# One core, two-layer encoder: the seventh product of a fast feed-forward chunk placed behind the second of the next

## The chip, the cores and the metric

The kernel runs on one core of a Trainium2 chip. The metric is device microseconds of one execution, from the reference's inputs in HBM to the output in HBM.

## What is computed

Two encoder layers on 1024 tokens of width 1024, all in float32. Each layer is a modulated RMS norm, an attention block with a gated residual, a second modulated RMS norm and a SwiGLU feed-forward block with a gated residual. What the change touches is the second half of a layer:

```python
def swiglu(h, w_in, w_out):
    gate, up = jnp.split(h @ w_in, 2, axis=-1)
    return (jax.nn.silu(gate) * up) @ w_out

x = x + gate2 * swiglu(h, f_w_in[i], f_w_out[i])     # h: 1024 x 1024, w_in: 1024 x 5632, w_out: 2816 x 1024
```

After layer 0 the next layer's first norm follows, after layer 1 the final norm.

## The kernel before, in words

**Arithmetic.** A float32 operand is held as a rounded half and the rest (`split`, L95): ScalarE casts the tile to its rounded half (L96), VectorE subtracts that from the tile (L97). A product of two operands is three TensorE matmuls (`mm3`, L99: hi x hi at L106, hi x lo at L107, lo x hi at L108), each over 512 columns. Activations are stored with the features on the partitions, so that a weight block is the stationary operand and 512 tokens are the moving one.

**First feed-forward matmul** (`ffn`, L847). Of the 22 chunks of 128 gate and 128 up features, the first two (LEAD) are computed directly by `plain` (L922), once for each half of the tokens, with four products of 12 matmuls each. The other 20 are computed by `fast` (L934), which takes both halves of the tokens at once with seven products of 12 matmuls instead of eight (a Strassen scheme: the four quarters are token half by half of the contraction against gate or up). A chunk so has 84 matmuls. The seven moving operands `ops[1..7]` are formed once by `norm_parts` (L754); the seven weight operands are formed for each chunk by `w_operands` (L806): four raw blocks of 128 x 512 come by DMA, named (1,1), (1,2) for gate and (2,1), (2,2) for up; GpSimd forms sums and differences of them (`comb`, L816, L817), and each operand is then split into a pair `whi`, `wlo`. Pool `rw` has 5 raw tiles (RAW), pool `rp` 4 pairs (RP). The difference for product 7 is written into a raw tile of its own (L825), so that a chunk takes five raw tiles; the other sums are written over a block.

**The order inside `fast`** is 1, 7, 6, 2, 5, 4, 3. Products 1, 6, 5, 3 are summed one after the other in one half of a PSUM tile "S" (two of them exist), 7 and 4 in its other half, 2 in a bank "T". Between them the running sum is read out: after 1 by ScalarE (L941), after 7 by ScalarE (L943), after 6 by ScalarE (L945), after 2 by VectorE (L947), after 5 by VectorE (L952), after 4 by VectorE (L954), after 3 by ScalarE with Silu (L958). `glu` (L917, L919) multiplies gate and up, and `keep` (L891) stores the results and, for every second chunk, four differences of them to `gd` in HBM (seven stores, L895, for two chunks). In layer 0 a step of the next layer's modulation (`ada_half`, L138: a raw tile by DMA, L148 on ScalarE, L150 on GpSimd, and row sums on TensorE at each end of eight) is put in after product 2 and after product 4.

**What sets the order on each engine.** Each engine works through its own queue in order. The queues' order is fixed when the program is built, by a scheduler that walks a simulated time: among the instructions that are ready it takes the one earliest in the program's text. `high_priority(offset=n)` lets an instruction count as n places earlier. Forming and splitting a weight operand has it (WAHEAD, 60); the read-outs L941 to L958 and the Silu and product of `plain` (L931, L919) have none. A tile of a pool is given out again when its last reader is done.

**Second feed-forward matmul.** Seven such products again (`product`, L1021), in the order 1, 2, 6, 7, 4, 5, 3, each over 11 slices of 12 matmuls; a slice loads and splits a weight block (`left`, L986) and an activation tile from `gd` (`right`, L1010). After product 4 the first token half is complete. `norm(0, ...)` (L1046) is called there, ahead of product 5: `norm_rb` (L195) sums the squares over the partitions with row sums on TensorE (L187), raises them to the power -1/2 on GpSimd (L203) and spreads them with TensorE again (L193). What remains of the norm (8 steps in layer 0, each L214, L216, L217; 4 in layer 1, `final`, L1096) is kept in `side`, and one is taken after every second slice.

Of the kernel before, what the change touches and what calls it, by code (L numbers as in the profile page):

```python
# [11 lines left out]
AF = mybir.ActivationFunctionType  # L12
ALU = mybir.AluOpType
AX = mybir.AxisListType

P = 128
S = 1024
# [3 lines left out]
CH = 512  # L21
# [10 lines left out]
EAHEAD = 60  # L32
# [7 lines left out]
NP = NF // 2  # L40
# [19 lines left out]
class Trunk:  # L60
# [38 lines left out]
    def mm3(self, ps, w, xs, n, w0=0, first=True, last=True, more=False):  # L99

        whi, wlo = w
        mm = self.nc.tensor.matmul
        for k in range(n):
            ws = slice((w0 + k) * P, (w0 + k + 1) * P)
            xh, xl = xs[k]
            mm(ps, lhsT=whi[:, ws], rhs=xh, start=first and k == 0 and not more, stop=False, skip_group_check=more)  # L106
            mm(ps, lhsT=whi[:, ws], rhs=xl, start=False, stop=False, skip_group_check=more)  # L107
            mm(ps, lhsT=wlo[:, ws], rhs=xh, start=False, stop=last and k == n - 1, skip_group_check=more)  # L108

    def mm_part(self, ps, w, xs, part):  # L110
        n = KT // PARTS
# [80 lines left out]
        for i in range(n):  # L192
            nc.tensor.matmul(ps[:, i * P:(i + 1) * P], lhsT=r[:, i:i + 1].to_broadcast([P, P]), rhs=self.ident, start=True, stop=True)  # L193

    def norm_rb(self, sq, n=4, ps=None):  # L195
        nc = self.nc
        if ps is None:
            ps = self.bank("A")
        self.rowsum(ps, sq, n)
        v = self.t(self.sp, "v8", [P, 4])  # L200
        nc.vector.tensor_scalar(out=v[:, :n], in0=ps[:, :n], scalar1=1.0 / D, scalar2=EPS, op0=ALU.mult, op1=ALU.add)
        r = self.t(self.sp, "r8", [P, 4])
        nc.gpsimd.tensor_tensor(out=r[:, :n], in0=v[:, :n], in1=self.nhalf[:, :n], op=ALU.pow)  # L203
        self.bcast(ps, r[:, :n], n)
        return ps

    def norm_apply(self, pool, xs, rb, av, bv, hs):
# [598 lines left out]
    def w_operands(self, layer, f):  # L806
# [12 lines left out]

        def get(i):  # L820
            hi, lo = self.w_pair()
            if i in (1, 2, 4, 8):
                t = blk(*{1: (1, 1), 2: (1, 2), 4: (2, 2), 8: (2, 1)}[i])
            elif i in (7, 9):
                t = self.t(self.rw, "raw", [P, CH])  # L825
                x, y = (blk(2, 1), blk(1, 1)) if i == 7 else (blk(1, 1), blk(1, 2))
            else:
                t = blk(2, 1) if i == 5 else blk(1, 1) if i == 6 else blk(1, 2)
                if i != 3:
                    x, y = blk(2, 1), blk(2, 2)  # L830
            with self.tc.high_priority(offset=WAHEAD):
                if i == 7:
                    comb(t, x, y, ALU.subtract)
                elif i == 9:
                    comb(t, x, y, ALU.add)
                elif i == 5 and 6 not in raw:
                    comb(t, x, y, ALU.add)
                elif i == 6:
                    raw[6] = comb(t, comb(x, x, y, ALU.add), t, ALU.subtract)
                self.split(hi, lo, t)  # L840
                if i == 2 and 6 in raw:
                    comb(t, t, raw[6], ALU.subtract)
            return hi, lo

        return get

    def ffn(self, layer, wo, xdst):  # L847
        nc, tc, a = self.nc, self.tc, self.a
        m = self.mods[layer]
        gate2 = m[5]  # L850
        with tc.tile_pool(name="hb", bufs=22, reuse_waits="tile") as hb, \
# [22 lines left out]
            for c in range(2):  # L874
                sq = wo.part_b(ft, wslot, c, todo)
# [9 lines left out]
            tt = nc.vector.tensor_tensor  # L885
# [28 lines left out]
            def prod(ps, i, w):  # L914
                self.mm3(ps, w, ops[i], 4, first=i in (1, 2, 7), more=i in (3, 4, 5, 6))

            def glu(f, c, x, y):  # L917
                t = g_tile()
                tt(out=t, in0=x, in1=y, op=ALU.mult)  # L919
                return lambda: keep(f, c, t)  # L920

            def plain(f, c):  # L922

                get = self.w_operands(layer, f)
                ps = self.t(self.pss, "S")
                for h, (i, j) in enumerate((((1, 1), (2, 2)), ((8, 1), (4, 2))) if c == 0 else (((9, 3), (1, 7)), ((8, 7), (5, 3)))):
                    o = ps[:, h * CH:(h + 1) * CH]
                    self.mm3(o, get(i[0]), ops[i[1]], 4, last=False)
                    self.mm3(o, get(j[0]), ops[j[1]], 4, first=False)
                t = f_tile()  # L930
                nc.scalar.activation(out=t, in_=ps[:, :CH], func=AF.Silu)  # L931
                return glu(f, c, t, ps[:, CH:])

            def fast(f):  # L934

                get = self.w_operands(layer, f)
                xz, y = self.t(self.pss, "S"), self.bank("T")
                x, z = xz[:, :CH], xz[:, CH:]
                gate1, up1, gate0, up0 = (f_tile() for _ in range(4))
                prod(x, 1, get(1))  # L940
                nc.scalar.copy(out=gate0, in_=x)  # L941
                prod(z, 7, get(7))
                nc.scalar.copy(out=up1, in_=z)  # L943
                prod(x, 6, get(6))
                nc.scalar.copy(out=up0, in_=x)  # L945
                prod(y, 2, get(2))
                tt(out=gate0, in0=gate0, in1=y, op=ALU.add)  # L947
                nc.scalar.activation(out=gate0, in_=gate0, func=AF.Silu)
                if ada:
                    ada.pop(0)()  # L950
                prod(x, 5, get(5))
                tt(out=up1, in0=up1, in1=x, op=ALU.add)  # L952
                prod(z, 4, get(4))
                tt(out=up0, in0=up0, in1=z, op=ALU.add)  # L954
                if ada:
                    ada.pop(0)()
                prod(x, 3, get(3))
                nc.scalar.activation(out=gate1, in_=x, func=AF.Silu)  # L958
                a, b = glu(f, 0, gate0, up0), glu(f, 1, gate1, up1)
                a()  # L960
                b()

            for c in range(2):
                for f in range(LEAD):
                    plain(f, c)()
                if c == 0:
                    for s in late:
                        s()
            for f in range(LEAD, NF):
                fast(f)  # L970
            if layer == 0:
                self.make_a(self.avec[1][0], self.sm[:, C_N1 + 8:C_N1 + 16], self.mods[1][1])

# [3 lines left out]
            box = [{}, {}]  # L977
            hn = [[None] * KT, [None] * KT]
            side = []
# [30 lines left out]
            def right(i, k):  # L1010
                t = self.hslot(F32)
                nc.sync.dma_start(out=t, in_=gd[i - 1, k])
                hl = self.hpair()
                with self.tc.high_priority(offset=WAHEAD):
                    self.split(*hl, t)
                return hl

            def term(ps, w, x, o, k, more):
                self.mm3(ps, [t[:, o:o + P] for t in w], [x], 1, first=k == 0 and not more, last=k == NP - 1, more=more)

            def product(i, ps):  # L1021
                for k in range(NP):
# [23 lines left out]
            def norm(c, ps):  # L1046

                rb = self.norm_rb(box[c]["sq"], ps=ps)
# [31 lines left out]
            ws = [(left(3, k, pair), right(3, k)) for k in range(NP)]  # L1080
            for n0 in (0, CH // 2):
# [9 lines left out]
                ps = self.t(self.pss, "S")[:, :CH]  # L1091
# [181 lines left out]
```

## Time and profile before

| | |
|---|---|
| median of 3 runs | 2824.42 us (2817.63 to 2833.84) |
| the profiled execution, its own time | 2822.26 us |
| its span, first to last instruction | 2820.5 us |
| busy in the span: TensorE matmul, weight load | 2570.1 us (91%), 2076.0 us (74%) |
| VectorE, ScalarE, GpSimd | 1783.6, 1255.5, 923.1 us |
| matmuls and weight loads | 12684 each |

PE is TensorE's matmuls, PEld its weight loads, DVE VectorE, ACT ScalarE, POOL GpSimd, SP SyncE (which issues the DMAs). The clock is the granted clock of TensorE as a share of 2.4 GHz. Matmuls overlap: a matmul of 512 columns is shown for about 0.39 us, and the next starts before it ends.

### The profile page before, as it was taken

To read this page: it belongs to the slowest core of one execution; us is meant where nothing else is said; L and a number is where in the kernel's file an instruction comes from. 1 tells how busy PE (TensorE), PEld (TensorE's weight loads), DVE (VectorE), ACT (ScalarE), POOL (GpSimd) and SP (SyncE) were. 2 spreads that over 40 slices of the span, in tenths; PEclk is the share of its full clock that TensorE was granted. 3 is DMA by queue.
4 is the path that set the end of the run, shared out by engine and by line. 5 is a ranking of instruction groups with operands and counts; after the bars stand their busy time and mean duration, and the time that the engine had idled before them with its cause. 6 is when DMAs were issued, how large, how long until landed. Compare 5 with 4: busy or idle time off the path is not lost. (4 is left out here: it accounts for less than half of the span.)

```text
span 2820.5 us, 35123 instructions
## 1 busy us (share of the span) xinstructions
PE 2570.1 (91%) x12684; PEld 2076.0 (74%) x12684; DVE 1783.6 (63%) x2736; ACT 1255.5 (45%) x2175; POOL 923.1 (33%) x614
## 2 busy tenths in 40 slices
PE   7799999999979888999998899999989989999998
PEld 5577777777767666677876688888767666767787
DVE  6777778777585444445855777676575444445776
ACT  5555555554353333333434465555453333333443
POOL 7644345431153333330000465442152222220001
PEclk9899999999999999999999999999999999999999
DMA  6211111112213233327654222212212222227663
GB/s 249 75 46 53 57 60 60 59 43 88 97 42 120 99 110 106 115 99 263 224 175 147 92 75 94 79 68 94 83 38 79 94 97 79 94 79 242 202 198 131
DMA packets 145630, 303.46 MB, mean 108 GB/s; under 512 B 16048, under 2 KB 18352, under 8 KB 145456
## 3 DMA queue, kind: packets, MB, share of 16 engines
q1 hardware_dynamic: 145456, 301.21, 31.0%
q8 instruction: 100, 1.64, 0.2%
q14 instruction: 74, 0.61, 0.1%
HBM read 245.05 MB, written 56.10 MB: 107 GB/s over the span
## 5 line engine op out<-in xcount | busy, mean ns | idle before, releaser
L97 DVE TENSOR_TENSOR wlo<-raw,whi 128x512 fp32r<-128x512 f32 x415 | 325.4, 786 | 335.9 <-ACT whi L96 331.3
L96 ACT CAST whi<-raw 128x512 fp32r<-128x512 f32 x415 | 256.1, 619 | 525.1 <-PE S L107 450.2
L106 PE MATMUL S<-h,whi 128*128 128x512 f32 x968 | 387.1, 400 | 49.4 <-DVE g L919 24.7
L817 POOL TENSOR_TENSOR raw<-raw,raw 128x512 f32<-128x512 f32 x168 | 242.5, 1444 | 532.2 <-DMA raw<-in_w_in 234.8
L107 PE MATMUL S<-h,whi 128*128 128x512 f32 x968 | 381.4, 394 | 4.5 <-DVE h L217 4.5
L108 PE MATMUL S<-h,wlo 128*128 128x512 f32 x968 | 380.8, 393 | 0.5 <-DVE wlo L97 0.5
L106 PE MATMUL M<-h,whi 128*128 128x512 f32 (+1 forms) x701 | 285.3, 407 | 9.6 <-ACT tmp L473 5.9
L108 PE MATMUL M<-h,wlo 128*128 128x512 f32 (+1 forms) x701 | 276.7, 395 | 1.0 <-POOL wlo L97 1.0
L107 PE MATMUL M<-h,whi 128*128 128x512 f32 (+1 forms) x701 | 277.5, 396 | 0.0
L106 PEld LDWEIGHTS S<-h,whi 128*128 128x128 f32 x968 | 183.9, 190 | 113.0 <-ACT whi L96 39.0
L96 ACT CAST pt<-T 128x512 fp32r<-128x512 f32 x256 | 145.6, 589 | 192.8 <-PE T L259 191.6
L183 POOL TENSOR_TENSOR ft<-ft,ft 128x512 f32<-128x512 f32 x48 | 69.0, 1438 | 479.2 <-ACT ft L179 458.1
L97 DVE TENSOR_TENSOR pt<-T,pt 128x512 fp32r<-128x512 f32 x256 | 172.0, 684 | 83.2 <-ACT pt L96 82.8
L106 PE MATMUL S<-hb,whi 128*128 128x512 f32 x432 | 173.7, 402 | 53.3 <-ACT ft L943 53.3
L107 PEld LDWEIGHTS S<-h,whi 128*128 128x128 f32 x968 | 184.1, 190 | 40.7 <-DVE h L217 4.9
L108 PEld LDWEIGHTS S<-h,wlo 128*128 128x128 f32 x968 | 184.0, 190 | 40.6 <-DVE wlo L97 1.2
L130 POOL TENSOR_TENSOR wraw<-wraw,cond 128x1024 f32<-128x1024 f32 x64 | 154.2, 2410 | 131.5 <-DMA wraw<-in_ada_t 112.8
L96 ACT CAST h<-h 128x512 fp32r<-128x512 f32 x166 | 102.1, 618 | 184.4 <-DMA h<-gd 183.4
L97 DVE TENSOR_TENSOR h<-h,h 128x512 fp32r<-128x512 f32 x166 | 126.3, 765 | 91.0 <-ACT h L96 90.7
L559 DVE TENSOR_REDUCE mx<-S 128x1 f32<-128x1024 f32 x128 | 150.3, 1216 | 39.1 <-PE S L551 39.1
L562 ACT ACTIVATE e<-S,mx 128x1024 f32<-128x1024 f32 x128 | 141.5, 1112 | 74.6 <-DVE mx L561 74.5
L273 PE MATMUL A<-pt,v 128*128 128x256 f32 x512 | 153.5, 300 | 22.7 <-DVE pt L97 22.7
(287 smaller groups left out, 5928.3 us busy)
## 6 DMA issues: line engine op xcount, KB each, us to landing
raw<-in_w_in SPq DMA_DIRECT2D x192, 256.0 KB, 2.7
gd<-g SPq DMA_DIRECT2D x154, 256.0 KB, 2.0
h<-gd SPq DMA_DIRECT2D x154, 256.0 KB, 3.9
raw<-in_w_out SPq DMA_DIRECT2D x154, 256.0 KB, 3.2
wraw<-in_ada_t SPq DMA_DIRECT2D x64, 512.0 KB, 3.2
wraw<-in_wqkvA SPq DMA_DIRECT2D x23, 512.0 KB, 3.2
hb<-in_w_out SPq DMA_DIRECT2D x44, 256.0 KB, 4.4
aq<-in_ada_s SPq DMA_DIRECT2D x16, 512.0 KB, 5.0
```

What stands on the lines that cost most here:

```text
L96: self.nc.scalar.copy(out=hi, in_=src)
L97: (eng or self.nc.vector).tensor_tensor(out=lo, in0=src, in1=hi.bitcast(F32), op=ALU.subtract)
L106: mm(ps, lhsT=whi[:, ws], rhs=xh, start=first and k == 0 and not more, stop=False, skip_group_check=more)
L107: mm(ps, lhsT=whi[:, ws], rhs=xl, start=False, stop=False, skip_group_check=more)
L108: mm(ps, lhsT=wlo[:, ws], rhs=xh, start=False, stop=last and k == n - 1, skip_group_check=more)
L130: nc.gpsimd.tensor_tensor(out=w, in0=w, in1=cond, op=ALU.mult)
L183: (eng or nc.gpsimd).tensor_tensor(out=box["sq"][:, ns], in0=box["sq"][:, ns], in1=sq[:, ns], op=ALU.add)
L273: mm(ps, lhsT=vh[:, ks], rhs=lo, start=False, stop=(k == KT - 1))
L559: nc.vector.tensor_reduce(out=mx, in_=ps, op=ALU.max, axis=AX.X, negate=True)
L562: nc.scalar.activation(out=e, in_=ps, func=AF.Exp, bias=mx, scale=1.0, accum_out=sums[c])
L817: nc.gpsimd.tensor_tensor(out=o, in0=x, in1=y, op=op)
```

## The change

1. `fast` is split: product 3 with its Silu, the Silu of the other gate, the two multiplications and `keep` become a function that the next chunk calls after its product 7 (the last chunk's is called at the end). The order of a chunk is then 1, 7, (3 of the chunk before), 6, 4, 2, 5. In layer 0 the two modulation steps go in after that 3 and after 4.
2. `w_operands` writes all sums over the four blocks: 7 over (1,1), 6 in two steps over (2,1) and (1,1), 3 over (1,2). A chunk takes four raw tiles; GpSimd still has four operations for a chunk.
3. The read-outs of `fast` and the Silu and multiplication of `plain` get `high_priority(offset=EAHEAD)` (60).
4. In the second matmul `norm(0, ...)` is called inside product 5 after slice 5; its row sums are ordered behind slice 1's last matmul and its spreading matmuls behind slice 3's (`issue_after` puts an instruction behind a given one on its engine). `side` gives one step after every slice from 7 of product 5 on, and after every slice of product 3.

```diff
-    def norm_rb(self, sq, n=4, ps=None):
+    def norm_rb(self, sq, n=4, ps=None, spots=None):
+        spots = [self.tc.issue_after(i.ins) for i in spots] if spots else [contextlib.nullcontext()] * 2
...
-        self.rowsum(ps, sq, n)
+        with spots[0]:
+            self.rowsum(ps, sq, n)
...
-        self.bcast(ps, r[:, :n], n)
+        with spots[1]:
+            self.bcast(ps, r[:, :n], n)
...
-            if i in (1, 2, 4, 8):
-                t = blk(*{1: (1, 1), 2: (1, 2), 4: (2, 2), 8: (2, 1)}[i])
-            elif i in (7, 9):
-                t = self.t(self.rw, "raw", [P, CH])
...
             with self.tc.high_priority(offset=WAHEAD):
                 if i == 7:
-                    comb(t, x, y, ALU.subtract)
+                    comb(blk(1, 1), blk(2, 1), blk(1, 1), ALU.subtract)
+                elif i == 6 or i == 5 and not both:
+                    comb(blk(2, 1), blk(2, 1), blk(2, 2), ALU.add)
                 elif i == 9:
-                    comb(t, x, y, ALU.add)
...
+                    comb(blk(1, 2), blk(1, 1), blk(1, 2), ALU.add)
+                if i == 6:
+                    comb(blk(1, 1), blk(1, 1), blk(2, 2), ALU.add)
+                self.split(hi, lo, blk(*{1: (1, 1), 2: (1, 2), 3: (1, 2), 4: (2, 2), 5: (2, 1), 6: (1, 1), 7: (1, 1), 8: (2, 1), 9: (1, 2)}[i]))
+                if i == 2 and both:
+                    comb(blk(1, 2), blk(1, 2), blk(1, 1), ALU.subtract)
...
-                nc.scalar.activation(out=t, in_=ps[:, :CH], func=AF.Silu)
-                return glu(f, c, t, ps[:, CH:])
+                with self.tc.high_priority(offset=EAHEAD):
+                    nc.scalar.activation(out=t, in_=ps[:, :CH], func=AF.Silu)
+                    return glu(f, c, t, ps[:, CH:])
...
-            def fast(f):
+            def fast(f, prev):
...
+                soon = lambda: self.tc.high_priority(offset=EAHEAD)
                 prod(x, 1, get(1))
-                nc.scalar.copy(out=gate0, in_=x)
+                with soon():
+                    nc.scalar.copy(out=gate0, in_=x)
                 prod(z, 7, get(7))
...
+                if prev:
+                    prev()
...
+                prod(x, 6, get(6))
...
                 prod(z, 4, get(4))
...
+                prod(y, 2, get(2))
...
+                prod(x, 5, get(5))
...
+                def last():
+                    prod(x, 3, get(3))
+                    with soon():
+                        nc.scalar.activation(out=gate1, in_=x, func=AF.Silu)
+                    nc.scalar.activation(out=gate0, in_=gate0, func=AF.Silu)
+                    a, b = glu(f, 0, gate0, up0), glu(f, 1, gate1, up1)
+                    a()
+                    b()
...
             for f in range(LEAD, NF):
-                fast(f)
+                prev = fast(f, prev)
+            prev()
...
-                        term(ps[n], w, x, n * P, k, i in (3, 4, 5, 6))
-                    if side and k % 2:
+                        ins = term(ps[n], w, x, n * P, k, i in (3, 4, 5, 6))
+                    ends.append(ins)
+                    if i == 5 and k == 5:
+                        side.extend(norm(0, self.t(self.pss, "S")[:, :CH], (ends[1], ends[3])))
+                    if side and (i != 5 or k > 6):
                         side.pop(0)()
...
-            side += norm(0, self.t(self.pss, "S")[:, :CH])
```

## Rows read from the trace of the kernel before

**Rows 1.** Windows: both loops, a dense stretch, the plain stages (x: instructions; then clock, DMA share, GB/s)

```profile
core 0: us, PE busy (x) PEld busy (x) DVE busy (x) ACT busy (x) POOL busy (x), PEclk, DMA share, GB/s
863.92:1294.26 430.34, 384.97 (x1628) 296.49 (x1628) 203.79 (x276) 152.78 (x263) 141.97 (x103) 1.00 0.32 111
2146.71:2570.35 423.64, 379.10 (x1596) 293.71 (x1597) 194.24 (x271) 133.43 (x233) 110.20 (x75) 1.00 0.27 95
1300.00:1400.00 100.00, 99.25 (x437) 81.53 (x436) 72.48 (x112) 40.62 (x72) 4.88 (x3) 1.00 0.75 249
817.04:857.30 40.26, 26.78 (x111) 21.38 (x109) 36.70 (x39) 19.00 (x33) 25.08 (x16) 0.87 0.21 72
2098.03:2140.08 42.05, 29.10 (x110) 22.91 (x109) 36.15 (x39) 18.80 (x32) 24.66 (x16) 0.80 0.18 63
```

**Rows 2.** Groups of PE: out<-in, shapes, count, busy us, mean ns, idle before and its releasers

```profile
L106 PE MATMUL S<-h,whi 128*128 128x512 f32 x968 | 387.1, 400 | 49.4 <-DVE g L919 24.7 <-ACT whi L96 21.3 <-ACT ft L941 1.6
...
L106 PE MATMUL S<-hb,whi 128*128 128x512 f32 x432 | 173.7, 402 | 53.3 <-ACT ft L943 53.3
...
L106 PE MATMUL T<-h,whi 128*128 128x512 f32 (+1 forms) x314 | 124.5, 404 | 28.3 <-ACT whi L96 20.6 <-DVE h L1035 4.6 <-ACT h L96 3.0
```

**Rows 3.** Timeline of PE, one chunk of layer 1 (start us, duration, instruction, [idle before <-releaser])

```profile
2145.30 0.39 PE L108 MATMUL S<-hb,wlo 128*128 128x512 f32 x1
2146.71 0.50 PE L106 MATMUL S<-hb,whi 128*128 128x512 f32 x1 [1.02 <-ACT ft L943]
2147.05 0.39 PE L107 MATMUL S<-hb,whi 128*128 128x512 f32 x1
...
2150.21 0.50 PE L106 MATMUL S<-h,whi 128*128 128x512 f32 x1 [0.48 <-ACT whi L96]
...
2159.17 0.50 PE L106 MATMUL T<-h,whi 128*128 128x512 f32 x1 [0.48 <-ACT whi L96]
```

**Rows 4.** Timeline of ACT, ahead of a gap that ends at 2257.39 on PE

```profile
2256.23 0.62 ACT L96 CAST whi<-raw 128x512 fp32r<-128x512 f32 x1 [1.09 <-PE S L107]
2256.76 0.58 ACT L943 COPY ft<-S 128x512 f32<-128x512 f32 x1
```

**Rows 5.** Waits of the SP queue: line <- releaser: us in total, times, longest us

```profile
SPq L800 <- DVE wlo L97: 452.1, 130, 42.2
...
SPq L895 <- DVE g L919: 170.9, 62, 5.8
```

**Rows 6.** Instructions on the tile raw: count, ns min/median/max, first and last start

```profile
L97 DVE TENSOR_TENSOR wlo<-raw,whi x415: 677/691/1807, 749.2 to 2779.5; 128x512 fp32r<-128x512 f32 x139
...
L817 POOL TENSOR_TENSOR raw<-raw,raw x168: 1266/1294/1822, 803.7 to 2559.4; 128x512 f32<-128x512 f32 x168
...
DMA to landing us min/median/max: 2.4/2.8/5.9
```

**Rows 7.** Timeline of PE, modulation row sums in a chunk of layer 0

```profile
1035.33 1.05 PE L187 MATMUL M<-ones,acc 128*128 128x1 f32 x8
```

**Rows 8.** Timeline of PE, start of the second plain stage of layer 0

```profile
829.73 0.79 PE L106 MATMUL S<-h,whi 128*128 128x512 f32 x1 [12.30 <-DVE g L919]
...
834.95 0.50 PE L107 MATMUL S<-hb,whi 128*128 128x512 f32 x1 [1.18 <-DVE hb L97]
```

**Rows 9.** Timeline of DVE there

```profile
829.00 1.27 DVE L919 TENSOR_TENSOR g<-ft,S 128x512 f32<-128x512 f32 x2
```

**Rows 10.** Timeline of PE, the norm's sums ahead of product 5 in layer 0, then in layer 1

```profile
1465.38 1.05 PE L187 MATMUL S<-ones,ft 128*128 128x1 f32 x8 [1.04 <-POOL ft L183]
1467.78 2.07 PE L193 MATMUL S<-ident,r 128*128 128x128 f32 x8 [1.35 <-POOL r L203]
1472.02 1.22 PE L106 MATMUL T<-h,whi 128*128 128x512 f32 x2 [2.17 <-ACT h L96]
...
2758.37 1.16 PE L193 MATMUL S<-ident,r 128*128 128x128 f32 x8 [0.78 <-POOL r L203]
```

**Rows 11.** The norm's VectorE steps: count, ns min/median/max, first and last start

```profile
L214 DVE SCALAR_TENSOR_TENSOR ft<-h,a,S x8: 734/742/747, 1470.0 to 1508.8; 128x512 f32<-128x512 f32 x8
```

More of the change, by code (lines that the diff above doesn't have):

```diff
@@ L107, in mm3 @@
             mm(ps, lhsT=whi[:, ws], rhs=xl, start=False, stop=False, skip_group_check=more)
-            mm(ps, lhsT=wlo[:, ws], rhs=xh, start=False, stop=last and k == n - 1, skip_group_check=more)
+            ins = mm(ps, lhsT=wlo[:, ws], rhs=xh, start=False, stop=last and k == n - 1, skip_group_check=more)
+        return ins
     def mm_part(self, ps, w, xs, part):
@@ L804, in w_pair, with w_operands @@
         return self.t(self.rp, "whi", [P, CH], F32R), self.t(self.rp, "wlo", [P, CH], F32R)
-    def w_operands(self, layer, f):
+    def w_operands(self, layer, f, both=True):
         nc = self.nc
@@ L821, in get @@
             hi, lo = self.w_pair()
-            if i in (1, 2, 4, 8):
-                t = blk(*{1: (1, 1), 2: (1, 2), 4: (2, 2), 8: (2, 1)}[i])
-            elif i in (7, 9):
-                t = self.t(self.rw, "raw", [P, CH])
[L826 to L830, printed above, removed]
             with self.tc.high_priority(offset=WAHEAD):
                 if i == 7:
-                    comb(t, x, y, ALU.subtract)
+                    comb(blk(1, 1), blk(2, 1), blk(1, 1), ALU.subtract)
+                elif i == 6 or i == 5 and not both:
+                    comb(blk(2, 1), blk(2, 1), blk(2, 2), ALU.add)
                 elif i == 9:
-                    comb(t, x, y, ALU.add)
[L836 to L842, printed above, removed]
+                    comb(blk(1, 2), blk(1, 1), blk(1, 2), ALU.add)
[4 more added lines that the diff above has]
+                    comb(blk(1, 2), blk(1, 2), blk(1, 1), ALU.subtract)
             return hi, lo
@@ L922, in plain @@
             def plain(f, c):
-                get = self.w_operands(layer, f)
+                get = self.w_operands(layer, f, False)
                 ps = self.t(self.pss, "S")
@@ L939, in fast @@
                 gate1, up1, gate0, up0 = (f_tile() for _ in range(4))
+                soon = lambda: self.tc.high_priority(offset=EAHEAD)
                 prod(x, 1, get(1))
-                nc.scalar.copy(out=gate0, in_=x)
+                with soon():
+                    nc.scalar.copy(out=gate0, in_=x)
                 prod(z, 7, get(7))
[L943 to L948, printed above, removed]
+                with soon():
+                    nc.scalar.copy(out=up1, in_=z)
+                if prev:
+                    prev()
                 if ada:
                     ada.pop(0)()
-                prod(x, 5, get(5))
-                tt(out=up1, in0=up1, in1=x, op=ALU.add)
+                prod(x, 6, get(6))
+                with soon():
+                    up = nc.scalar.copy(out=up0, in_=x)
                 prod(z, 4, get(4))
-                tt(out=up0, in0=up0, in1=z, op=ALU.add)
+                with soon():
+                    tt(out=up0, in0=up0, in1=z, op=ALU.add)
                 if ada:
                     ada.pop(0)()
[L957 to L961, printed above, removed]
+                prod(y, 2, get(2))
+                with soon():
+                    tt(out=gate0, in0=gate0, in1=y, op=ALU.add)
+                prod(x, 5, get(5))
+                with soon():
+                    tt(out=up1, in0=up1, in1=x, op=ALU.add)
+                def last():
+                    prod(x, 3, get(3))
+                    with soon():
+                        nc.scalar.activation(out=gate1, in_=x, func=AF.Silu)
[3 more added lines that the diff above has]
+                    b()
+                return last
             for c in range(2):
@@ L968, in ffn @@
                         s()
+            prev = None
             for f in range(LEAD, NF):
-                fast(f)
+                prev = fast(f, prev)
+            prev()
             if layer == 0:
@@ L1018, in term @@
             def term(ps, w, x, o, k, more):
-                self.mm3(ps, [t[:, o:o + P] for t in w], [x], 1, first=k == 0 and not more, last=k == NP - 1, more=more)
+                return self.mm3(ps, [t[:, o:o + P] for t in w], [x], 1, first=k == 0 and not more, last=k == NP - 1, more=more)
             def product(i, ps):
+                ends = []
                 for k in range(NP):
@@ L1044, in y_banks, with norm @@
                 return [u[:, h * CH:(h + 1) * CH] for u in t for h in range(2)]
-            def norm(c, ps):
-                rb = self.norm_rb(box[c]["sq"], ps=ps)
+            def norm(c, ps, spots=None):
+                rb = self.norm_rb(box[c]["sq"], ps=ps, spots=spots)
                 if layer == 0:
```

## The prediction

> **What bounds the kernel now.** I read the windows first, to see which engine is full in the stage that the change touches. In the two loops over fast chunks [rows 1] nothing but TensorE is near full: VectorE is busy in 204 of 430 us and 194 of 424, ScalarE and GpSimd less. TensorE's clock is whole (1.00), so what is lost there is waiting. How much: between the first and the last product 6 of a layer lie 19 chunk periods, 430.34 and 423.64 us, or 22.65 and 22.30 us a chunk of 84 matmuls (1628 records are 19 x 84 and 32 row sums, 1596 are 19 x 84). A stretch of the second matmul, with the same tiles and four pairs, starts 437 matmuls in 100 us at the same clock [rows 1]: 0.2288 us from start to start, 2.75 us a product, 19.22 us a chunk. So each chunk has some 3.1 us that a fed TensorE would not need.
>
> The timeline of PE shows where [rows 3]: three gaps a chunk, alike in all 40. The largest, 1.02 us here and 1.3 on average (53.3 us over 40 [rows 2]), stands ahead of product 6 and ends with L943, the read-out of product 7; the two others, 0.48 us each, end with the cast of a weight. A gap costs more than it shows, since the last start lies 1.41 us before the next (1.18 lost) and the one after comes 0.34 us later (0.11 lost): 1.29 for 1.02. The groups [rows 2] say that this is the rule and no accident: 53.3 us behind L943, 21.3 and 20.6 behind casts, 1.6 behind L941.
>
> Why product 6 waits for another product's read-out: the timeline of ACT [rows 4] has the cast ahead of the read-out, both at the moment when product 7 ends, and product 6 comes directly behind 7 on PE. The text has 2 behind 6; by the tiles' names in the timeline PE's real order is 6, first two matmuls of the next chunk's 1, 5, rest of 1, 4, beginning of 2, 3, rest of 2, next 7. Product 2 is late because its raw block is: raw loads wait 452 us in the SP queue for a tile whose last reader is a split [rows 5]. With five raw tiles taken by each chunk nothing can be fetched ahead.
>
> **The change, part by part.**
>
> *Order.* Product 3 of the chunk before now stands between 7 and 6, and 4 and 2 between 6 and 5. Every read of a running sum gets one or two products (2.75 or 5.5 us) where now it can have none; a cast and a read-out, 0.62 and 0.58 us [rows 4], fit in either order. The 53.3 us and their restarts go. Next late would be the weights.
>
> *Raw tiles.* Four for each chunk out of five: block (1,2) stays until the next chunk's 3, the fifth tile takes the next chunk's first block once that split is over, about 16 us early by the order of products; landing takes 2.8 us, 5.9 at most [rows 6]. In layer 0 two modulation tiles a chunk use the same pool, each for a landing, a scaling and an addition, about 5 us if these take what a cast and a sum take [rows 4, 6]; that leaves every load ahead of its split by my count of the frees.
>
> *Pairs.* Four pairs at one product each: a cast can start when the product four places back ends, 8.2 us before its own product. The in-place sums make a chain: split 1, sum, split 7, sum, cast 6. With the medians [rows 4, 6] that is 0.62 + 0.69 + 1.29 + 0.62 + 0.69 + 1.29 + 0.62 = 5.8 us, with the longest ones 9.1; product 6 starts three products behind 1, and 1's cast lies at least one before it, so 11.0 us are there. GpSimd has four sums as before, so its time costs nothing more. VectorE's and ScalarE's work is unchanged.
>
> *What moves with 3.* Its 12 matmuls, two Silus, two multiplications, two subtractions a chunk and 3.5 stores move past the next chunk's first raw loads. The stores hold the SP queue for 171 us in all [rows 5]; behind loads they hold back less. The results are read by the second matmul only, the last pair in its slice 10 (10 x 2.75 us on), so lateness there is covered; without that cover a chunk's lateness would show once per layer, under 3 us. At the end of each loop 3 follows 5 with one read-out by VectorE between (about 0.7 us, a split's length [rows 6]); the second matmul's first slices are there to fill that.
>
> The loops' sum: 853.98 us less 38 x 19.22 = 730.4, less four groups of row sums in layer 0 of 1.05 us [rows 7], which stay: 119.4 us at most. What remains as gaps the trace can't show; it lies between nothing and one cast gap a chunk (0.48 + 0.27 = 0.75 us). I take 0.2, since the dense stretch is nearer to the new order than the loops are: 7.6 us. Gain 111.8. The first chunk of a layer lies ahead of the periods and loses one gap less: 2 x 1.29 = 2.6.
>
> By TensorE's busy time the loops seem to have only 45.4 + 44.5 = 89.9 us to give [rows 1]. The Trainium skill, "Perfetto Trace Analysis", section "Identifying the Most-Contended Engine", says that matmul busy time is no measure of the room left and that the weight loads' busy share is: 69% here against 81.5% in the dense stretch, which gives 130 us. The trace agrees with the page, as a matmul of 0.39 us covers a gap of its own; by busy time the total below would be about 2732.
>
> *Read-outs of the plain stage.* PE waits 12.30 us in layer 0 [rows 8], 24.7 in both [rows 2], for L919, which VectorE reaches at 829.00 [rows 9], behind norm work. With priority it comes up to 12 us sooner. But VectorE is busy in 36.7 of 40.3 us there [rows 1], and PE is stopped again at 834.95 by a split of VectorE [rows 8], which the two earlier multiplications push back by 1.2 us. Upper bound: 110 matmuls at 0.2288 are 25.2 us, so the stages lose 40.26 + 42.05 - 50.4 = 32 us in all, with the low clock (0.87, 0.80). Lower bound: 2.5 us lost. Before that split PE can do three of four slices of two products, 18 matmuls or 4.1 us; less 1.2, twice: 5 us gained.
>
> *Norm.* In layer 0 PE stands 1.04, 1.35 and 2.17 us around the norm's sums [rows 10], and the sums and the matmuls behind them run at a lower clock; 0.78 in layer 1. Pinned between slices they find their inputs ready: 5 to 9 us gained. Against that a step of 2 x 0.74 us [rows 11] now falls on each slice, beside two or three splits of 0.69: 2.9 to 3.6 us of VectorE in 2.75, for eight slices up to 6 us late. I take 3 gained, between -6 and +9.
>
> Sum: 111.8 + 2.6 + 5 + 3 = 122.4. The profiled execution took 2822.3, so 2699.9; the median of the runs is 2.1 above it: **2702**.
>
> **Rivals.**
>
> *Only the read-out gap goes.* The scheduler again begins products before their weights are split, and the two cast gaps stay. For it: the four pairs are unchanged, and the queue is ordered by simulated time. Against: late raw blocks were what disturbed the order. Gain 53.3 + 40 x 0.27 = 64, and 8 from the other parts: 2752.
>
> *The change doesn't do what it says.* The text's order is no command: 2 already runs behind 5 and 4. If 7 ends up directly ahead of 6 again, only the 8 us of the other parts remain: 2816, within 0.5%.
>
> *Slower: the moved product holds a pair.* The operand of 3 is ready as soon as 2 is split; if it is cast at once, it keeps one of four pairs over 5, 1 and 7, and the next 1 may take another. Then casts come when a product ends, and each of seven products waits 0.75 us as at today's cast gaps: 5.2 us a chunk against 3.1, 40 x 2.1 = 84 more, 2908; with five gaps a chunk about 2848. It decides from five gaps on. Against it: the second matmul runs dense with four pairs.
>
> **How the numbers follow.** About 0.5% (14 us) is what a measurement of this kernel can tell from no change. Chances: the forecast 0.71, only the read-out gap 0.17, no change 0.06, slower 0.06. So faster 0.88, same 0.06, slower 0.06. The forecast's own range: with no gap left, the whole plain stage and the norm's upper end it would be 41 us lower (2661), which won't come all together: 2672. On the other side the range takes in the first rival with the lower ends of plain stage and norm, 2752 + 13: 2765. Below lies perhaps 0.05, above 0.14.
>
> **What would show it.** Right: product 6 behind 3 on PE, no idle behind L943, product 6 to product 6 at 19.2 to 19.6 us, weight loads busy about 80% in the loops, SP's wait for splits far shorter, row sums inside product 5. Wrong: cast gaps still standing (first rival), a T product out of place, GpSimd's sums or raw loads as releasers of casts, or a period above 22 us. The weakest term is the order that the scheduler makes of the new text.

## The result, and the profile after

The changed kernel takes 2704.21 us (median of 4 runs, 2701.76 to 2706.90), the kernel before 2828.28 us beside it (4 runs, 2817.63 to 2833.84): a ratio of 0.9566, with a 95% interval from 0.9533 to 0.9599. The forecast was 2702. The profiled execution took 2701.94 us, its span is 2699.8 us, 120.7 less than before.

The windows of the kernel after, in the columns of [rows 1]: 18 chunk periods of layer 0, 17 of layer 1, and the two plain stages.

```profile
core 0: us, PE busy (x) PEld busy (x) DVE busy (x) ACT busy (x) POOL busy (x), PEclk, DMA share, GB/s
...
882.09:1231.79 349.70, 348.01 (x1546) 286.89 (x1544) 208.35 (x260) 142.03 (x247) 138.44 (x98) 1.00 0.36 128
2103.32:2427.43 324.11, 324.11 (x1430) 267.40 (x1429) 191.81 (x237) 117.01 (x205) 103.70 (x69) 1.00 0.29 103
817.50:858.92 41.42, 27.94 (x111) 22.25 (x109) 35.89 (x39) 20.69 (x36) 25.32 (x17) 0.84 0.19 70
2040.60:2081.41 40.81, 27.27 (x109) 21.92 (x109) 35.96 (x40) 18.95 (x34) 23.85 (x16) 0.83 0.18 62
```

A chunk takes 19.43 us in layer 0 and 19.07 in layer 1, where it took 22.65 and 22.30 [rows 1]; in the second window PE is busy without a break. The weight loads are busy for 82.0% and 82.5% of these windows, as in the dense stretch of the kernel before. The plain stages, 41.42 and 40.81 us, took 40.26 and 42.05: nothing gained there.

The groups of PE in the kernel after, in the columns of [rows 2]:

```profile
L106 PE MATMUL S<-h,whi 128*128 128x512 f32 x968 | 375.5, 395 | 34.5 <-DVE g L915 26.1 <-ACT whi L96 5.4 <-ACT ft L941 1.7
...
L106 PE MATMUL S<-hb,whi 128*128 128x512 f32 x432 | 169.3, 392 | 1.1 <-ACT ft L944 0.8
...
L106 PE MATMUL T<-h,whi 128*128 128x512 f32 (+1 forms) x314 | 118.9, 397 | 10.4 <-DVE h L1053 4.9 <-ACT h L96 4.3 <-ACT whi L96 1.0
```

PE's order is not the text's (1, 7, 3 of the chunk before, 6, 4, 2, 5). The starts of one stretch of layer 1 in the kernel after:

```profile
2114.20 0.39 PE L106 MATMUL S<-h,whi 128*128 128x512 f32 x1
...
2116.92 0.39 PE L106 MATMUL S<-h,whi 128*128 128x512 f32 x1
...
2119.64 0.39 PE L106 MATMUL S<-hb,whi 128*128 128x512 f32 x1
...
2122.36 0.39 PE L106 MATMUL T<-h,whi 128*128 128x512 f32 x1
...
2122.81 0.39 PE L106 MATMUL S<-h,whi 128*128 128x512 f32 x1
```

These are product 7, then 5 of the chunk before, 6, two matmuls of 2, and only then 3 of the chunk before. Products 4, 5 and 6 can be told by the tiles of their four slices (hb, hb, h, hb; h, h, hb, hb; hb, hb, h, h), 7 and 3 by their read-outs. So what stands between 7 and 6 is a product of the other tile S, but it is 5 and not 3.

All three gaps of a chunk are gone. Behind the read-out of product 7 (L944 here) 0.8 us is left of 53.3, behind casts 5.4 of 21.3 and 1.0 of 20.6; 4.4 of the 5.4 are one wait at the start of attention, where before had 3.0. What stays is the wait for the plain stage's multiplication, L915 here: 26.1 us, 24.7 before.

**Where the time went**, by laying the same matmul of both traces side by side. From the first product 2 of the loop to the end of the second matmul's product 1, layer 0 became 62.4 us shorter (857.30 to 1333.80 became 858.92 to 1273.01) and layer 1 63.3 us: 125.7 in all. What lies behind that in layer 0, up to the start of attention, became 4.3 us longer, in layer 1, up to the end, 1.3 us. Ahead of the loop layer 0 is 1.6 us longer, layer 1 from attention on 2.2 us shorter.

### The profile page after: what moved, and what is told of

It reads as the page before. It is cut to its first block, busy times and chain, and to the rows that moved or that the text cites. A ratio compares the mean times of both kernels' runs of the same rounds, so it can differ in the third digit from the quotient of the medians.

```text
span 2699.8 us, 35007 instructions
## 1 busy us (share of the span) xinstructions
PE 2540.6 (94%) x12684; PEld 2088.3 (77%) x12684; DVE 1822.4 (68%) x2736; ACT 1254.0 (46%) x2175; POOL 931.8 (35%) x614
## 5 line engine op out<-in xcount | busy, mean ns | idle before, releaser
L106 PE MATMUL S<-h,whi 128*128 128x512 f32 x968 | 375.5, 395 | 34.5 <-DVE g L915 26.1
L107 PE MATMUL S<-h,whi 128*128 128x512 f32 x968 | 381.3, 394 | 4.8 <-DVE h L222 4.5
```

## The experiments

Two readings of the two cast gaps stood against each other. **A**, the prediction's: raw blocks come late, so weights are cast late; the new order removes the read-out gap, the in-place sums the cast gaps. **R1**: the order removes all three, the sums nothing. Later a third, **W**, asked why an order should do that.

### One part of the change undone

`a2_raw_old` puts the sums back as they were (five raw tiles a chunk):

```diff
-                    comb(blk(1, 1), blk(2, 1), blk(1, 1), ALU.subtract)
+                    comb(t, x, y, ALU.subtract)
...
-                self.split(hi, lo, blk(*{1: (1, 1), 2: (1, 2), 3: (1, 2), 4: (2, 2), 5: (2, 1), 6: (1, 1), 7: (1, 1), 8: (2, 1), 9: (1, 2)}[i]))
+                self.split(hi, lo, t)
```

> The changed kernel with the weight sums of before (product 7's difference in a raw tile of its own, five raw tiles a chunk); order, priorities and norm as changed. Theory A (the order takes the gap behind the read-out of product 7, the freed raw tile takes the two cast gaps): no idle behind the read-out, two gaps of about 0.48 us behind casts in each chunk, 40 x 2 x 0.75 = 60 us more than the changed kernel, about 2764. Rival R1 (the order alone does it): within 8 us of 2704.

2704.63 us against 2831.4 of the kernel before on that chip: 0.955 (0.9531 to 0.9569). Nothing is lost without the in-place sums. A falls.

`a4_order_old` puts the order 1, 7, 6, 2, 5, 4, 3 back (with its places for the modulation steps and for the Silu of the first gate) and keeps all else:

```diff
-                if prev:
-                    prev()
+                prod(x, 6, get(6))
...
+                prod(y, 2, get(2))
...
-                prod(x, 6, get(6))
+                prod(x, 5, get(5))
...
-                def last():
-                    prod(x, 3, get(3))
+                prod(x, 3, get(3))
```

> The changed kernel with the order 1, 7, 6, 2, 5, 4, 3 of before; in-place sums, priorities and norm as changed. Theory A: cast gaps stay away, product 6 stands directly behind 7 and waits about 1 us for its read-out: 64 us more, about 2768. Rival R2 (the raw tile alone does it, because the scheduler can then put 2 between): within 8 us of 2704. Rival R3 (priority puts the read-out ahead of the cast): a gap of about 0.6 us ahead of 6, 25 to 30 us more, about 2732.

2837.05 us, 1.0026 (1.0012 to 1.004): the whole gain is gone and a little more, which none of the three expectations had. Its groups of PE:

```profile
L106 PE MATMUL S<-h,whi 128*128 128x512 f32 x968 | 390.0, 403 | 70.3 <-ACT whi L96 43.9 <-DVE g L915 26.3
...
L106 PE MATMUL S<-hb,whi 128*128 128x512 f32 x432 | 175.3, 406 | 44.7 <-ACT ft L944 44.7
```

The gaps of before are back, behind casts with 43.9 us where [rows 2] have 21.3, although a chunk takes four raw tiles and the read-outs have priority.

`a3_prio_old` takes the priorities of the read-outs and of the plain stage away:

```diff
-                with self.tc.high_priority(offset=EAHEAD):
-                    nc.scalar.activation(out=t, in_=ps[:, :CH], func=AF.Silu)
-                    return glu(f, c, t, ps[:, CH:])
+                nc.scalar.activation(out=t, in_=ps[:, :CH], func=AF.Silu)
+                return glu(f, c, t, ps[:, CH:])
...
-                soon = lambda: self.tc.high_priority(offset=EAHEAD)
+                soon = contextlib.nullcontext
```

> The changed kernel without priority for the read-outs of the fast and the plain chunks; order, in-place sums and norm as changed. Theory A (two products lie between a sum and its reader, so a late read-out costs nothing): within 8 us of 2704. Rival R3 (the priority takes away the read-out gaps): 40 to 64 us more, 2744 to 2768.

2705.36 us, 0.9553 (0.9534 to 0.9571): they are worth nothing that can be measured.

`a1_norm_old` has the norm's sums ahead of product 5 again and a step after every second slice:

```diff
-                    if i == 5 and k == 5:
-                        side.extend(norm(0, self.t(self.pss, "S")[:, :CH], (ends[1], ends[3])))
-                    if side and (i != 5 or k > 6):
+                    if side and k % 2:
...
+            side += norm(0, self.t(self.pss, "S")[:, :CH])
```

> The changed kernel with the norm called ahead of product 5 and a step after every second slice, as before. By the two traces between the same matmuls the second matmul of layer 0 became 4 us longer and the tail of layer 1 6 us longer. Theory N1 (the pinned norm costs this): 4 to 10 us less than the changed kernel, 2694 to 2700. Rival N2 (as the prediction's sum had it): 3 us more, about 2707. Rival N3 (chance of DMA timing): the same within 2 us.

2707.62 us, 0.9563 (0.9544 to 0.9582). On the same chip that is 2.3 to 3.0 us above the two runs beside it, less than the interval's half width of some 5 us: the pinned sums may be worth the 3 us of the forecast, or nothing.

### One part of the change alone

`b1_order_only` is the kernel before with the new order of `fast` (with its places for the modulation steps and for the Silu of the first gate) and nothing else:

```diff
                 prod(z, 7, get(7))
                 nc.scalar.copy(out=up1, in_=z)
+                if prev:
+                    prev()
                 prod(x, 6, get(6))
...
-                prod(y, 2, get(2))
+                prod(z, 4, get(4))
...
-                prod(x, 5, get(5))
+                prod(y, 2, get(2))
...
-                prod(z, 4, get(4))
+                prod(x, 5, get(5))
...
+                def last():
                     prod(x, 3, get(3))
```

> The kernel of before with the new order alone (product 3 behind the next chunk's 7, then 6, 4, 2, 5); weight sums, priorities and norm as before. Theory A: the gap behind the read-out of 7 goes, cast gaps stay: 60 to 64 us less than before, about 2762. Rival R1 (the order alone does it): about 2705. Rival R3 (without priority the read-outs stay late): within 14 us of before.

2709.32 us against 2832.38: 0.9564 (0.9547 to 0.9581). The order alone is the change. Its groups of PE:

```profile
L106 PE MATMUL S<-h,whi 128*128 128x512 f32 x968 | 372.8, 394 | 28.7 <-DVE g L924 24.6 <-ACT whi L96 2.5 <-ACT h L221 1.6
...
L106 PE MATMUL S<-hb,whi 128*128 128x512 f32 x432 | 169.3, 392 | 3.4 <-ACT ft L959 3.4
```

And its longest wait of the SP queue, in the columns of [rows 5]:

```profile
SPq L805 <- DVE wlo L97: 413.3, 165, 40.2
```

The raw loads still wait 413 us for splits, 452 before, and hardly a matmul is the later for it: 2.5 us of these matmuls' waiting end with a cast. The long wait of that queue, on which A rested, was a queue that runs as far ahead as its tiles let it.

`b2_raw_only` is the kernel before with the in-place sums alone (the diff of `a2_raw_old` the other way round).

> The kernel of before with the in-place weight sums alone; order, priorities and norm as before. Theory A: the two cast gaps go, the gap ahead of 6 stays: about 60 us less than before, 2765. Rival R1: within 14 us of before. Rival R2 (the raw tile alone does it): about 2705.

2838.67 us, 1.0028 (1.0015 to 1.004): slower by a little. Its groups of PE, then two of its waits:

```profile
L106 PE MATMUL S<-h,whi 128*128 128x512 f32 x968 | 389.1, 402 | 70.4 <-ACT whi L96 43.6 <-DVE g L915 26.2 <-DVE h L1042 0.7
...
L106 PE MATMUL S<-hb,whi 128*128 128x512 f32 x432 | 175.8, 407 | 44.9 <-ACT ft L943 44.9
```

```profile
ACT whi L96 <- POOL raw L822: 99.3, 43, 3.8
...
PE T L106 <- ACT whi L96: 18.1, 38, 0.5
```

The three gaps sum to 43.6 + 44.9 + 18.1 = 106.6 us, 95.2 before [rows 2]. A cast now waits for the sums over its block, 99.3 us in 43 times; the trace of before has 5.0 us of that in 4. The chain of splits and sums, which the prediction found shorter than its cover, is not always covered in the old order; in the new one the same wait (110.0 us in the kernel after) leaves next to no gap in the loops. The loss is all in layer 0: there the stretch from the first product 2 to the end of the second matmul's product 1 is 21.8 us longer than before, in layer 1 it is 5.2 us shorter. Layer 0 has the modulation tiles in the same pool; whether they are the reason was not tried.

### Why the order does it

In the trace of before the weights of products 5, 4 and 3 are cast 11 to 14 us ahead of their first matmul, if casts come in the order in which the text asks for them; only those of 1 and 2, of which two matmuls run early, are cast just before them. So raw blocks did not come late. The kernel before at one such gap, PE, then DVE, then ACT (the casts of the weights of product 3 and of the next chunk's product 2):

```profile
2247.04 0.39 PE L108 MATMUL S<-hb,wlo 128*128 128x512 f32 x1
2247.91 0.50 PE L106 MATMUL T<-h,whi 128*128 128x512 f32 x1 [0.48 <-ACT whi L96]
2248.25 0.40 PE L107 MATMUL T<-h,whi 128*128 128x512 f32 x1
2248.49 0.39 PE L106 MATMUL S<-h,whi 128*128 128x512 f32 x1
```

```profile
2247.47 0.69 DVE L954 TENSOR_TENSOR ft<-ft,S 128x512 f32<-128x512 f32 x1 [1.55 <-PE S L108]
```

```profile
2234.33 0.60 ACT L96 CAST whi<-raw 128x512 fp32r<-128x512 f32 x1
...
2247.24 0.62 ACT L96 CAST whi<-raw 128x512 fp32r<-128x512 f32 x1 [2.04 <-PE S L107]
```

Product 4 ends, two matmuls of the next chunk's 2 run once their cast is done, and 3 starts at 2248.49, shortly after the read-out of 4 (L954, to 2248.16), though 4 is summed in the other half of the tile and 3's weight was cast 14 us ago. The cast at 2247.24 starts when the matmuls of product 4 that use `whi` end, so it had waited for a pair; casts do so in `e1_z_bank` below as well, and there PE doesn't wait for them.

W: the program keeps track of a whole tile "S", so any product in either half waits for the read-out of the product before it in that tile. Ahead of 6 the trace shows this itself, as PE is released by L943, which reads the other half [rows 3]. Ahead of 3 (behind 4, the other half) and of 5 (behind 6, the same half) it is a reading: a gap of one read-out, into which the queue puts the first two matmuls of another product; they start when a cast ends, and so give the gap the cast's name. 3 and 5 follow directly on those two matmuls, so the trace can't tell whether they would have had to wait without them.

It does show that product 2 is not late. The product 2 that stands around 3 is the next chunk's: in the first chunk of layer 0 product 2 starts at 857.30, ahead of 7 (860.02) and 6 (863.92) of the same chunk.

`e1_z_bank` takes products 7 and 4 out of the shared tile, in the text's old order:

```diff
-                x, z = xz[:, :CH], xz[:, CH:]
+                x, z = xz[:, :CH], self.bank("A")
```

> The kernel of before, order and all, with products 7 and 4 summed in the PSUM bank A instead of the second half of the tile S. Theory W (the three gaps are one cause: two sums share a tile, so a product on S waits for the read-out of whichever product on S came before it, and what was read as a wait for a cast is a filler put into that pause): with a tile of its own for 7 and 4 every read-out has another product beside it in the old order too; no idle behind read-outs or casts, about 110 to 125 us less than before, 2705 to 2720. Rival P (weights: late raw blocks and four pairs make the cast gaps): the gap behind the read-out of 7 goes, the two cast gaps stay, about 64 us less, 2767. Rival 0 (the scheduler's order stays the bound): within 14 us of before.

2723.22 us against 2831.4: 0.9631 (0.96 to 0.9663). One line, nothing moved in the text, 108 us; W had 2705 to 2720. Its groups of PE (products 7 and 4 now write A):

```profile
L106 PE MATMUL S<-h,whi 128*128 128x512 f32 x808 | 311.7, 399 | 37.0 <-DVE g L919 24.7 <-ACT h L96 6.8 <-ACT whi L96 5.3
...
L106 PE MATMUL S<-hb,whi 128*128 128x512 f32 x272 | 106.9, 393 | 0.0
...
L106 PE MATMUL A<-hb,whi 128*128 128x512 f32 x160 | 62.2, 389 | 0.0
```

No idle behind a read-out of 7, and 5.3 us behind casts, with the same raw tiles and pairs: P falls, and the cast gaps go with the shared tile, as W has it. But the expectation's "in the old order too" doesn't hold on PE, since the scheduler reckons with the tiles. The starts of four products in layer 1 of `e1_z_bank`:

```profile
2154.84 0.39 PE L106 MATMUL A<-h,whi 128*128 128x512 f32 x1
...
2157.56 0.39 PE L106 MATMUL S<-h,whi 128*128 128x512 f32 x1
...
2160.28 0.39 PE L106 MATMUL T<-h,whi 128*128 128x512 f32 x1
...
2163.00 0.39 PE L106 MATMUL S<-hb,whi 128*128 128x512 f32 x1
```

They are 7, 3 of the chunk before (its Silu, L958, follows at 2160.78), 2 and 6; then come 4 and 5. So with a tile of its own for 7 and 4 the scheduler itself moved 3 behind the next chunk's 7, much as the change does by hand. Whether PE's old order with separate tiles would be as fast no run shows.

The loops are not what `e1_z_bank` lacks against the order (108 us against 123 in `b1_order_only`): its period in layer 1 is 19.04 us. By its profiled execution it loses behind them, from the end of the second matmul's product 1 on: 203.4 us to the start of attention in layer 0, where before had 187.5, and 222.5 us to the end in layer 1, where before had 206.9. Why was not followed up.

`b3_move_only` is `b1_order_only` with only product 3 moved: the others stay 6, 2, 5, 4.

```diff
-                prod(z, 4, get(4))
-                with soon():
-                    tt(out=up0, in0=up0, in1=z, op=ALU.add)
                 prod(y, 2, get(2))
...
                     tt(out=up1, in0=up1, in1=x, op=ALU.add)
+                prod(z, 4, get(4))
+                with soon():
+                    tt(out=up0, in0=up0, in1=z, op=ALU.add)
```

> The kernel of before with product 3 moved behind the next chunk's 7, and the rest in the old order 6, 2, 5, 4; nothing else changed. Theory W: the move makes two S tiles alternate, so that all three gaps can be filled from the other chunk, the swap of 2, 5 and 4 adds little: within 15 us of the order alone, 2705 to 2720. Rival M (6, 2, 5, 4 keeps 5 and 4 next to each other on one tile, so one read-out of 0.7 us and its restart is seen in each chunk): 40 x 0.9 = 36 us more, about 2745.

2757.8 us, 0.9758 (0.9727 to 0.979): 74 of the 123 us, short of both expectations (2705 to 2720, 2745). One gap a chunk is left. PE there:

```profile
2220.63 0.39 PE L108 MATMUL T<-hb,wlo 128*128 128x512 f32 x1
2221.82 0.50 PE L106 MATMUL S<-h,whi 128*128 128x512 f32 x1 [0.81 <-ACT ft L975]
2222.16 0.39 PE L107 MATMUL S<-h,whi 128*128 128x512 f32 x1
```

ACT at that time in the same kernel, then in the kernel after:

```profile
2220.66 0.62 ACT L96 CAST whi<-raw 128x512 fp32r<-128x512 f32 x1 [1.93 <-PE S L107]
2221.18 0.59 ACT L975 ACTIVATE ft<-S 128x512 f32<-128x512 f32 x1
```

```profile
2220.86 0.62 ACT L96 CAST whi<-raw 128x512 fp32r<-128x512 f32 x1 [2.55 <-PE S L107]
2221.39 0.59 ACT L967 ACTIVATE ft<-S 128x512 f32<-128x512 f32 x1
```

ScalarE does the same in both: a cast, then product 3's Silu (L975, L967). In `b3_move_only` product 1 of the chunk after the next, which takes over that very tile, stands behind 3 with one matmul into T between, and waits. With 4 ahead of 2 the rest of product 2, ten matmuls into T, stands between, and the same read-out costs nothing. A start lies 1.19 us after the last one and the next 0.34 us on, where 0.23 each is dense: 1.07 us lost, 43 for 40 chunks, most of the 49 us that the old places of 2, 5 and 4 cost.

### The plain stage

PE stands 13.00 us in the kernel after, as before 12.30 [rows 8], for L915. Is it the Silu's result tile, the queue of VectorE, or the norm work itself? `c1_plain_tile` gives the Silu a tile of another pool; `c2_kmajor_tile` also computes the four products slice by slice, so that PE needs only the first slices of the norm's operands; `d1_dve_norm` takes the changed kernel and moves the norm's GpSimd work to VectorE; `d2_dve_kmajor` has the tile and the slice order on top of that.

```diff
-                t = f_tile()
+                t = self.t(aa, "acc", [P, CH])
...
+                for k in range(4):
+                    for n, (i, j) in enumerate(terms):
...
+                        self.mm3(o, ws[n], ops[j][k:k + 1], 1, k, first=n % 2 == 0 and k == 0, last=n % 2 == 1 and k == 3)
...
-            sub(e, e, h0[d], nc.gpsimd)
-            put(5, e, nc.gpsimd)
+            sub(e, e, h0[d])
+            put(5, e)
...
-            sub(t, h0[d], t, nc.gpsimd)
+            sub(t, h0[d], t)
```

> The changed kernel, with plain's Silu written to the pool of the modulation's sum instead of the pool ft. Theory T (the 13 us wait stays because the Silu's tile comes behind the norm steps' tiles in the pool ft, not because of its priority): the wait for the multiplication goes, the matmuls of the second plain stage begin 10 us sooner and stop at VectorE's last split of the norm; 3 to 8 us less, about 2698. Rival V (VectorE decides when the multiplication comes, whatever the tile): the 13 us wait stays, within 3 us of 2704.

> As c1_plain_tile, and plain's four products go slice by slice (first slice of all four, then the second) instead of product by product. If theory T holds and the stage then waits for the norm's slices one by one, 36 of 48 matmuls of the first chunk are done before the last slice comes: 8 us less in each layer, about 2688. If VectorE is the bound whatever the order: as c1_plain_tile, within 3 us.

> The changed kernel with the subtractions that norm_parts gives to GpSimd (the operands 5 and 6, and the split of 5) on VectorE. In the second plain stage VectorE's instructions beside GpSimd's take 1.75 us instead of 0.69. Theory C (this overlap makes the norm late, and with it the multiplication that frees S): 10 instructions shorten by 1.06 us and 8 to 12 of 0.69 are added, so that PE's 13 us wait becomes 8 to 10 in each layer; 6 to 10 us less than the changed kernel, about 2697. Rival V (VectorE's sum of work decides): no change or up to 6 us more, 2704 to 2710.

> As d1_dve_norm, with the Silu's tile and the slice by slice order of c2_kmajor_tile. Theory C: S is free early, the slices come in VectorE's pace and PE works between them; 12 to 18 us less than the changed kernel, about 2690. Rival V: as c2_kmajor_tile, 2702 to 2708.

They took 2709.65 us (0.9568, 0.9549 to 0.9588), 2705.08 (0.9547, 0.953 to 0.9565), 2702.63 (0.9554, 0.9532 to 0.9577) and 2708.18 (0.9568, 0.9543 to 0.9594). None can be told from the changed kernel, so theories T and C, by which 3 to 18 us go, fail. The wait only changed its name. PE in `c1_plain_tile`, then in `c2_kmajor_tile`, then in `d1_dve_norm`:

```profile
835.26 0.77 PE L106 MATMUL S<-h,whi 128*128 128x512 f32 x1 [14.25 <-ACT hb L96]
```

```profile
824.94 0.76 PE L106 MATMUL S<-h,whi 128*128 128x512 f32 x1 [7.21 <-ACT hb L96]
...
832.66 0.51 PE L108 MATMUL S<-h,wlo 128*128 128x512 f32 x1 [2.69 <-DVE wlo L97]
```

```profile
833.83 0.80 PE L106 MATMUL S<-h,whi 128*128 128x512 f32 x1 [10.60 <-DVE g L915]
```

With the tile free the first matmul waits for an operand of the norm instead, and no shorter; in slice order PE starts 6 us earlier, stops again, and the stage ends no earlier. So where the read-out stands is not the bound. That the norm's own work on VectorE and the engines beside it is, the releasers suggest; no run has less of that work.

## Why the prediction was right, point by point

- **Loops**: forecast 111.8 + 2.6 = 114.4 us, measured 125.7. The bound was sound: the period is the dense stretch's 19.22 us, a little above in layer 0, which has the row sums, and below in layer 1. The residual of 0.2 us a chunk (7.6 us) was too much; layer 1 has none. Where the other 3.7 us come from was not followed up.
- **Read-out gap**: 53.3 us gone, as said, since another product stands between 7 and 6. It is not the one that was forecast: on PE it is 5 of the chunk before, and 3 comes after 6. That read-outs and casts "fit in either order" is what `a3_prio_old` shows.
- **The step that failed: raw tiles and pairs.** "Product 2 is late because its raw block is" was read from the SP queue's wait of 452 us [rows 5] and from the releaser's name on two gaps. Product 2 runs early, ahead of 7 and 6 of its chunk. `a2_raw_old` and `b1_order_only` show that the five tiles were enough, `b2_raw_only` that the four alone cost 0.28%, `e1_z_bank` that all three gaps go with the shared tile, with weights as before. That the sum came out is luck in this part: it priced the gaps away, whichever part removed them; the forecast of `b2_raw_only` from this step was wrong by its sign.
- **Its signs**: no idle behind the read-out of 7, the period, the loads' 82% and the row sums inside product 5 came. Product 6 behind 3 did not, nor did the far shorter wait of SP: it waits 317.2 us for splits and another 156.6 for sums, where it waited 452.1 for splits.
- **First rival (only the read-out gap goes, 2752)**: it stood on the cast gaps having a cause of their own, and they had none. `b3_move_only` comes to 2757.8, but its remaining gap is a read-out of 3.
- **Slower, by a pair that is held**: not seen; 1.0 and 5.4 us behind casts.
- **Plain stage**: forecast 5 us gained, measured nothing. The multiplication did not come up: VectorE reaches it at 830.13 behind the same norm work, and in the four kernels a free tile, another slice order or less GpSimd work moves PE's wait and does not shorten the run.
- **Norm**: forecast 3 us gained. `a1_norm_old` allows for that; by the traces the stretch from the second matmul's product 1 on lost 4.3 + 1.3 us, inside the range of -6 to +9 that was given. The pinned sums don't seem to be what lost it: from that product's end to a group of 16 row sums in attention, layer 0 takes 299.9 us before, 304.7 in the kernel after, and 308.2 and 309.3 in `b1_order_only` and `a1_norm_old`, which have the new order with the old norm. These are single executions, and other kernels with the pinned sums lie between 301.2 and 309.1, so the size stays open.
- So the sum's 122.4 us and the measured 124.1 agree because the loops gave 11 us more and the other stretches about that much less, by the plain stage's 5 us and by the stretches behind the loops, which became 5.6 us longer and not 3 shorter.
- The range's upper end, 2752 + 13, is a slip: with the lower ends named for the plain stage (2.5 us lost) and the norm (6 lost), against 5 and 3 gained, it is 2752 + 16.5. Nothing hangs on it.

By TensorE's busy time the loops had 89.9 us to give, by the weight loads' share 130; they gave 125.7. The Trainium skill, "Perfetto Trace Analysis", section "Identifying the Most-Contended Engine", asks for the second reading, and the trace agrees. The same page, section "Matmuls", says that independent matmul groups should rotate through PSUM banks so that one's read-out lies beside the next one's matmuls; `e1_z_bank` agrees with its 108 us, though what it shows is a tile that the program tracks as one, and a scheduler that finds another order once it is two.

## What to carry to other kernels

The releaser's name on a gap tells who was last, not why the engine was free to wait: look at what ran ahead of the gap and whether the matmuls behind it belong there, and look at how early the operands that were not named are ready. Two running sums in the halves of one PSUM tile are one buffer to the program that plans the queues; put an unrelated product between a sum and the next use of its tile, or give it a tile of its own. The text's order is not the engine's: read a product's place from the trace, by its operands and read-outs, before a wait is explained by it. A long wait in a DMA queue is no cost until a computing engine is shown waiting for that transfer.

## What had not been expected of the hardware

Many of VectorE's subtractions and splits of 128 x 512 in the plain stage take 1.75 us, as its timeline in the kernel after shows, and 0.68 us once GpSimd's part of the norm is gone, as in `d1_dve_norm` at the same place:

```profile
826.79 1.75 DVE L97 TENSOR_TENSOR h<-ft,h 128x512 fp32r<-128x512 f32 x1
828.45 1.75 DVE L776 TENSOR_TENSOR g<-ft,ft 128x512 f32<-128x512 f32 x1
830.13 1.27 DVE L915 TENSOR_TENSOR g<-ft,S 128x512 f32<-128x512 f32 x2
```

```profile
831.89 0.68 DVE L97 TENSOR_TENSOR h<-ft,h 128x512 fp32r<-128x512 f32 x1
832.49 0.68 DVE L776 TENSOR_TENSOR g<-ft,ft 128x512 f32<-128x512 f32 x1
833.10 1.27 DVE L915 TENSOR_TENSOR g<-ft,S 128x512 f32<-128x512 f32 x2
```

GpSimd is busy for 25 us of that stage in the kernel after, and many of VectorE's steps beside it take more than twice as long. Moving the norm's part onto VectorE shortens PE's wait from 13.00 to 10.60 us and no more; VectorE then has that work to do. The Trainium skill, "SBUF — State Buffer", section "Who interferes with whom", states a cause: a VectorE instruction with two SBUF inputs contends with a GpSimd instruction that reads SBUF, because its second input comes through a read interface that the two engines share, and with at most one SBUF input it does not. The trace agrees: L915, with one input in PSUM, takes 1.27 us for two in both kernels.
